# Attention scores of one transformer layer on one core: two score blocks at a time, with the product of high parts done as two half-height matmuls

## The chip, the cores and the metric

The kernel runs on one core of a Trainium2 chip. A core has a matrix engine (PE; its weight loads are listed apart as PEld), a vector engine (DVE), a scalar engine (ACT), a small general engine (POOL), and a sequencer (SP) that does nothing here but issue DMAs. Each works through its own list of instructions in order, and they wait for each other by semaphores. PE reads its operands from the 128 partitions of the on-chip memory and writes its results into banks of 128 partitions by 512 float32.

The metric is the device time of one execution, in microseconds (us). Before the change it is 1014.34 us, the median of three runs (1014.22 to 1014.41).

## The reference

One layer with 1024 tokens and a width of 1024, all in float32, cut to what matters here:

```python
hn = rmsnorm(x, norm_mix)
qa, ka, va, qb, kb, vb = split(hn @ w_in)          # head size 64
# A: 8 query heads in 2 groups, one key head a group; |i - j| <= 128
s = q_i @ k_i.T / 8                                 # a block of 128 queries, up to 384 keys
s = where(valid, s, -1e30); m = max(max(s), sink)
p = exp(s - m); o = (p @ v) / (sum(p) + exp(sink - m))
# B: 8 heads over a 16 x 64 grid of tokens, window 8 x 16, learned bias
p = softmax(q_r @ k_win / 8 + bias); o = p @ v_win
h = x + concat(rmsnorm(o_a), rmsnorm(o_b)) @ w_out
h = h + (silu(conv3(rmsnorm(h) @ w_gate)) * (rmsnorm(h) @ w_up)) @ w_down
out = rmsnorm(h)
```

## The kernel before

**Numbers in two parts.** PE multiplies numbers of a reduced float32 format (`fp32r`). To keep float32's precision, a number is split into a high part, which is the number in that format, and a low part, which is the rest. A product of two matrices of 128 rows is then three matmuls: high by high, low by high, high by low (`block`, lines 190 to 192, on the tiles `xgh`, `xgl`, `whi`, `wlo`). A head is only 64 numbers deep, half of PE's 128 rows. So for the scores one tile holds high and low part of the same 64 rows on top of each other: a query tile `q` has high above low, the key tile `ka` one of the two orders and `kb` the other. Two full-height matmuls of `q` with the two key tiles, added up in one bank, give high by high, low by low, high by low and low by high.

**Stages.** The projections `hn @ w_in` run as 18 jobs (`Project`), and eight jobs (`OutA`) are the first half of the output projection. Beside these jobs runs the attention: first A (16 units: 2 groups by 8 blocks of 128 queries), then B (8 heads, each in 4 units with 8 blocks in all). After it come the rest of the output projection, and the gated MLP with its products in a seven-product scheme, to the end.

**What a score goes through.** `scores` (line 397) takes a bank of tag `s`, of which there are two, and issues the two matmuls of line 404 for one block of 128 queries of one head: 384 key columns, or 256 for the first and the last block. `softmax` (line 423) follows: DVE reads the bank, adds mask or bias, and takes the row's extreme `nm` (line 435, called the eviction below: when it ends, the bank is free); ACT takes the exponential (line 443); DVE the reciprocal of the sum (line 445); POOL scales (line 447). Two blocks share one tile `p` and one reciprocal: in A they are two query heads of one group on the same block, in B two neighbouring blocks of one head. Later, `t_step` transposes `p` on PE (lines 483 and 559), ACT and DVE split it (lines 457 and 458), and `v_step` multiplies by the values (lines 489, 490, 570, 571).

**Order.** PE's order is written out by hand. A loop over the units emits transposes, score steps (`q_step`) and value steps, with scores about two units ahead, and after each of them a number of projection blocks set by the table `RATES`. The other engines' order is made by a scheduler from priorities, so that it moves when the code does.

**Stacks.** In B, `split_qk` (line 307) scales and splits a tile that has 64 rows of queries above 64 rows of keys into `ka` (high) and `kb` (low). DMAs on SP's queue then copy the two query parts into `q` (lines 316 and 317), after which the freed upper halves of `kb` and `ka` are overwritten with the keys' high and low parts (lines 318 and 319). In A, `split_first`, `split_pair`, `split_first_k` and `split_k` do the like; there the two query heads of a pair already have their parts stacked in opposite orders, except in `split_pair`.

Of the kernel before, what the change touches and what calls it, by code (L numbers as in the profile page):

```python
# [58 lines left out]
def hybrid_layer(tc, xT, w_first, w_in, w_out, w_gate, w_up, w_down, small, sink, rpb, consts, rope, out):  # L59
    nc = tc.nc  # L60
    with ExitStack() as ctx:
# [32 lines left out]
        f32 = lambda ap: ap.bitcast(F32)  # L94
# [184 lines left out]
        def split_pair(t):  # L279

            a, b = big("q", "op", F32R), big("q", "op", F32R)
            lo = t[:, :].bitcast(F32R)
            for h in range(2):
                nc.scalar.activation(a[:, tsl(h)], t[:, tsl(h)], AF.Copy, scale=-HD ** -0.5)
                nc.vector.scalar_tensor_tensor(lo[:, tsl(h)], t[:, tsl(h)], -HD ** -0.5, f32(a[:, tsl(h)]), op0=ALU.mult, op1=ALU.subtract)
            nc.sync.dma_start(f32(b[0:64, :]), f32(a[64:128, :]))
            nc.sync.dma_start(f32(b[64:128, :]), t[64:128])
            nc.sync.dma_start(f32(a[64:128, :]), t[0:64])
            return [a, b]

# [17 lines left out]
        def split_qk(t):  # L308

            a, b, q = big("ka", "op", F32R), big("kb", "op", F32R), big("q", "op", F32R)  # L310
            by = cst[:, K_SCALE:K_SCALE + 1]
            for h in range(2):
                nc.scalar.activation(a[:, tsl(h)], t[:, tsl(h)], AF.Copy, scale=by)
                nc.vector.scalar_tensor_tensor(b[:, tsl(h)], t[:, tsl(h)], by, f32(a[:, tsl(h)]), op0=ALU.mult, op1=ALU.subtract)
            with tc.high_priority(offset=500):
                nc.sync.dma_start(f32(q[0:64, :]), f32(a[0:64, :]))
                nc.sync.dma_start(f32(q[64:128, :]), f32(b[0:64, :]))
                mark["stacked"] = nc.sync.dma_start(f32(b[0:64, :]), f32(a[64:128, :]))
                nc.sync.dma_start(f32(a[0:64, :]), f32(b[64:128, :]))
            return q, (a, b)  # L320

        def split_k(t, e):

            a, b = big("ka", "op", F32R), big("kb", "op", F32R)
            o = 64 - e
            nc.scalar.activation(a[e:e + 64], t[e:e + 64], AF.Copy)
            nc.sync.dma_start(f32(b[o:o + 64, :]), f32(a[e:e + 64, :]))
            nc.vector.tensor_tensor(b[e:e + 64], t[e:e + 64], f32(a[e:e + 64, :]), op=ALU.subtract)
            nc.sync.dma_start(f32(a[o:o + 64, :]), f32(b[e:e + 64, :]))
            return a, b  # L330

        later = []

# [61 lines left out]
        def near(b):  # L395
            return [c for c in (b - 1, b, b + 1) if 0 <= c < NB]

        def scores(q, k, b):
            cs = near(b)
            n = 128 * len(cs)  # L400
            ps = bank("s", "s")
            qs = q[:, b * 128:(b + 1) * 128]
            for i in range(2):
                nc.tensor.matmul(ps[:, 0:n], qs, k[i][:, cs[0] * 128:cs[0] * 128 + n].rearrange("p (s w) -> p w s", s=2), start=i == 0, stop=i == 1)  # L404
            return ps, n

        pairs = [0]
        w2 = lambda ap: ap.rearrange("p (s w) -> p s w", s=2)

# [10 lines left out]
                with tc.high_priority(offset=50):  # L420
                    deferred.pop(0)(*order)

        def softmax(st, j, ps, n, bias, nsink=None):

            exponentials()
            w = lambda ap: ap.rearrange("p (s w) -> p s w", s=2)
            p = st["p"]
            with tc.high_priority(offset=50):
                nm = spool.tile([128, 1], F32, name="nm")
                if j == 0:  # L430
                    st["sm"], st["n"] = spool.tile([128, 2], F32, name="sm"), [n, n]
                sm, st["n"][j] = st["sm"], n
                if nsink is not None and j == 0:
                    nc.gpsimd.tensor_copy(p[:, 0:2, n:n + 1], nsink.rearrange("p (j o) -> p j o", o=1))
                nc.vector.tensor_tensor_reduce(  # L435
                    out=w(p[:, j, 0:n]), in0=ps[:, 0:n].rearrange("p (w s) -> p s w", s=2), in1=bias, scale=1.0, scalar=3e38 if nsink is None else nsink[:, j:j + 1],
                    op0=ALU.add, op1=ALU.min, accum_out=nm)
                e = n if nsink is None else n + 1
                widths = list(st["n"])

                def finish(*order):
                    with behind(*order):
                        nc.scalar.activation(p[:, j, 0:e], p[:, j, 0:e], AF.Exp, bias=nm, scale=-1.0, accum_out=sm[:, j:j + 1])  # L443
                    if j == 1:
                        nc.vector.reciprocal(sm, sm)  # L445
                        for i, m in enumerate(widths):
                            mark["scaled"] = nc.gpsimd.tensor_scalar(p[:, i, 0:m], p[:, i, 0:m], sm[:, i:i + 1], 1.0, op0=ALU.mult, op1=ALU.mult)  # L447

                deferred.append(finish)
                if nsink is None:  # L450
                    exponentials()
# [9 lines left out]
        def unit_window(g, b):  # L461

            cs, n = near(b), 128 * len(near(b))
            ps4 = [None] * 4
            mask = w2(cst[:, K_MA + 128 * (cs[0] - b + 1):K_MA + 128 * (cs[-1] - b + 2)])
            st = {}

            def q_step(j):
                def go():
                    if j % 2 == 0:  # L470
                        st["p"] = pair_tile(True)
                    ps, _ = scores(qa[g, j // 2][j % 2], ka[g], b)
                    softmax(st, j % 2, ps, n, mask, nsink[:, 4 * g + j - j % 2:4 * g + j - j % 2 + 2])
                    ps4[j] = st["p"][:, j % 2, :]
                return go

            def t_step(i):
                def go():
                    if i == 0:
                        st["o"] = bank("o", "o")  # L480
                    pt = bank("pt", "pt")
                    for j in range(4):
                        nc.tensor.transpose(pt[:, j * 128:(j + 1) * 128], ps4[j][:, i * 128:(i + 1) * 128], ident)  # L483
                    ph, pl = split_pt(pt, HALF)
                    exponentials("high")

                    def v_step():
                        o, v = st["o"], va[g]
                        nc.tensor.matmul(o, v[:, cs[i], :], mv(ph[:, :]), start=i == 0, stop=False)
                        nc.tensor.matmul(o, v[:, cs[i], :], mv(pl[:, :]), start=False, stop=i == len(cs) - 1)  # L490
                        if i == len(cs) - 1:
                            leave()
                    return v_step
                return go

            def leave():
                ot = apool.tile([128, 2, 128], F32, name="ot", tag="ot", bufs=1, padded_shape=[128, 4, 128])
                o4 = pv(st["o"][:, :])
                halved = lambda ap: ap.rearrange("p (s w) -> p s w", s=2)
                for e in range(2):  # L500
                    me, other = slice(64 * e, 64 * e + 64), slice(64 - 64 * e, 128 - 64 * e)
                    nc.scalar.activation(ot[me].rearrange("p j (s w) -> p j s w", s=2), o4[other, e::2], AF.Copy)
                    for i in range(2):
                        if mix[2 * g + i] is None:
                            mix[2 * g + i] = big("mixa", "mix")
                        nc.vector.tensor_tensor(halved(mix[2 * g + i][me, b * 128:(b + 1) * 128]), o4[me, e + 2 * i], halved(ot[me, i, :]), op=ALU.add)

            return [q_step(j) for j in range(4)], [t_step(i) for i in range(len(cs))]
# [20 lines left out]
        def units_grid(h):  # L529
# [6 lines left out]
            def q_step(b):  # L536
                def go():
                    if b == 0:
                        bias_of[h] = bias_of.pop(h, None) or bias_tiles(h)
                    if b == 4 and h < 7:  # L540
                        bias_of[h + 1] = bias_tiles(h + 1)
                    x = bias_of[h]
                    if b % 2 == 0:
                        st["p"] = pair_tile()
                    sel = slice(2, 5, 2) if b == 0 else slice(0, 3, 2) if b == NB - 1 else slice(1, 4)
                    ps, n = scores(qb[h], kb[h], b)
                    softmax(st, b % 2, ps, n, x[:, sel, :] if n == 256 else w2(x[:, sel, :].rearrange("p c w -> p (c w)")))
                    ps4[b] = st["p"][:, b % 2, :]
                return go
# [1172 lines left out]
```

## Time and profile before

| | before |
|---|---|
| median of three runs | 1014.34 us (1014.22 to 1014.41) |
| span of the profiled execution | 1012.1 us |
| outside the span (difference of these two) | 2.2 us |
| PE busy | 1004.5 us, 99% of the span |
| weight loads, DVE, ACT, POOL busy | 88%, 82%, 55%, 10% |
| granted clock of PE | 0.998 of full |
| score matmuls (line 404) | 256, from 52.1 to 330.4 us |

The profile comes from one execution, of which the span from the first to the last instruction is known; nothing else of that execution's own time is given, so the span stands for it. A timeline row gives start, length, engine, line, operation and tiles. PE's matmuls overlap in their pipeline and the ends given are modelled: a row of 0.38 us is followed by the next one 0.22 us later. So what a matmul costs is read from the distance between two starts, not from the length. A "busy" of 99% says likewise only that PE's list never ran dry.

### The profile page before, as it was taken

Reading aid. Unit: us, or ns where it says so; the run is one execution under the profiler, and the core shown is the slowest. Engines: PE = TensorE matmul, PEld = TensorE weight load, DVE = VectorE, ACT = ScalarE, POOL = GpSimd, SP = SyncE. Lnnn points to the kernel's source line nnn. Section 1 sums busy time; section 2 is a strip of 40 time slices with the busy share of each in tenths; the row PEclk is TensorE's granted clock in tenths of the full one; section 3 lists DMA queues with packets and bytes.
Section 4 is the critical chain, followed back from the end, with each engine's and each line's share of the span. In section 5 each row is a group of like instructions: output and inputs, shape, how many; then the busy total and the mean of one; then the engine's idle time right before and its main releaser. Section 6 shows DMA issues by size and latency. Waiting matters only on the chain.

```text
span 1012.1 us, 14835 instructions
## 1 busy us (share of the span) xinstructions
PE 1004.5 (99%) x5080; PEld 888.4 (88%) x5080; DVE 834.7 (82%) x1570; ACT 561.0 (55%) x1080; POOL 101.6 (10%) x186
## 2 busy tenths in 40 slices
PE   9999999999999999999999999999999999999997
PEld 8899898899899888888888888888888888888887
DVE  7899887768888799999987786786777678996675
ACT  8567776658687554565544443443444645554451
POOL 0233342222322100000000000000000000000001
PEclk9999999999999999999999999999999999999999
DMA  7223022333334366232552333323332799976654
GB/s 296 83 79 90 32 73 63 84 84 83 95 94 136 126 205 220 74 103 64 195 187 90 112 115 115 105 94 115 104 119 90 239 315 329 306 241 231 214 174 177
DMA packets 68524, 145.46 MB, mean 144 GB/s; under 512 B 8280, under 2 KB 18784, under 8 KB 68448
## 3 DMA queue, kind: packets, MB, share of 16 engines
q1 hardware_dynamic: 58360, 119.27, 36.9%
q10 hardware_dynamic: 10088, 25.24, 6.4%
q8 instruction: 40, 0.66, 0.3%
q14 instruction: 36, 0.29, 0.1%
HBM read 104.11 MB, written 28.58 MB: 131 GB/s over the span
## 4 chain that ended last, share of the span: by engine, by line
PE 93%; DVE 3%; ACT 2%; DMA 1%; issue 1%; SPq 0%; DVEq 0%; ACTq 0%
PE x L1059 8%; PE x L1057 8%; PE x L1058 8%; PE pj L190 7%; PE pj L192 7%; PE pj L191 7%; PE dn L1059 7%; PE dn L1058 7%; PE dn L1057 7%; PE y L1059 4%; PE y L1057 4%; PE y L1058 4%; PE s L404 3%; PE pt L483 2%; PE z L1057 2%; PE z L1059 2%
## 5 line engine op out<-in xcount | busy, mean ns | idle before, releaser
L1057 PE MATMUL x<-hg,whi 128*128 128x512 f32 x352 | 133.5, 379 | 0.0
L1058 PE MATMUL x<-hg,whi 128*128 128x512 f32 x352 | 133.4, 379 | 0.0
L1059 PE MATMUL x<-hg,wlo 128*128 128x512 f32 x352 | 133.4, 379 | 0.0
L1057 PE MATMUL dn<-xd,whi 128*128 128x512 f32 (+1 forms) x330 | 120.8, 366 | 0.0
L1058 PE MATMUL dn<-xd,whi 128*128 128x512 f32 (+1 forms) x330 | 120.5, 365 | 0.0
L1059 PE MATMUL dn<-xd,wlo 128*128 128x512 f32 (+1 forms) x330 | 120.5, 365 | 0.0
L1031 ACT ACTIVATE whi<-ws 128x512 fp32r<-128x512 f32 (+1 forms) x100 | 60.9, 623 | 76.0 <-DVE ws L1171 14.5
L443 ACT ACTIVATE p<-p,nm 128x385 f32<-128x385 f32 (+3 forms) x128 | 75.2, 588 | 45.8 <-DVE nm L435 43.1
L190 PE MATMUL pj<-xgh,whi 128*128 128x512 f32 x245 | 99.7, 407 | 0.2 <-DVE v L346 0.2
L447 POOL TENSOR_SCALAR p<-p,sm 128x384 f32<-128x384 f32 (+1 forms) x128 | 76.4, 610 | 195.9 <-DVE sm L445 161.7
L191 PE MATMUL pj<-xgl,whi 128*128 128x512 f32 x245 | 92.9, 379 | 0.0
L192 PE MATMUL pj<-xgh,wlo 128*128 128x512 f32 x245 | 92.9, 379 | 0.0
L1031 ACT ACTIVATE whi<-raw 128x512 fp32r<-128x512 f32 (+1 forms) x102 | 61.2, 612 | 49.9 <-PE x L1058 14.9
L1032 DVE TENSOR_TENSOR wlo<-ws,whi 128x512 fp32r<-128x512 f32 (+1 forms) x100 | 66.8, 683 | 20.0 <-ACT whi L1031 19.6
L458 DVE TENSOR_TENSOR pl<-pt,ph 128x384 fp32r<-128x384 f32 (+2 forms) x108 | 63.4, 587 | 17.5 <-ACT ph L457 16.5
L1057 PEld LDWEIGHTS x<-hg,whi 128*128 128x128 f32 x352 | 66.5, 189 | 9.4
L1058 PEld LDWEIGHTS x<-hg,whi 128*128 128x128 f32 x352 | 66.5, 189 | 9.4
L1059 PEld LDWEIGHTS x<-hg,wlo 128*128 128x128 f32 x352 | 66.5, 189 | 9.4
L1032 DVE TENSOR_TENSOR wlo<-raw,whi 128x512 fp32r<-128x512 f32 (+1 forms) x102 | 66.8, 672 | 6.2 <-ACT whi L1031 6.1
L1532 POOL TENSOR_TENSOR h<-h,wide 128x256 f32<-128x256 f32 x4 | 2.8, 731 | 671.2 <-ACT wide L1528 671.2
L457 ACT ACTIVATE ph<-pt 128x384 fp32r<-128x384 f32 (+2 forms) x108 | 55.4, 513 | 26.3 <-PE pt L483 14.2
L1057 PEld LDWEIGHTS dn<-xd,whi 128*128 128x128 f32 x330 | 62.5, 189 | 7.8
(276 smaller groups left out, 2504.2 us busy)
## 6 DMA issues: line engine op xcount, KB each, us to landing
xd<-x SPq DMA_DIRECT2D x77, 256.0 KB, 4.9
raw<-in_w_down_dram SPq DMA_DIRECT2D x72, 256.0 KB, 4.6
raw<-in_w_gate_dram SPq DMA_DIRECT2D x22, 512.0 KB, 3.5
raw<-in_w_up_dram SPq DMA_DIRECT2D x22, 512.0 KB, 3.8
x<-c ACTq DMA_DIRECT2D x22, 512.0 KB, 2.8
raw<-in_w_in_dram SPq DMA_DIRECT2D x30, 256.0 KB, 2.8
raw<-in_w_down_dram SPq DMA_DIRECT2D x36, 192.0 KB, 4.2
x<-t ACTq DMA_DIRECT2D x11, 512.0 KB, 2.6
```

What stands on the lines that cost most here:

```text
L190: nc.tensor.matmul(ps, w[0], mv(x[0][:, tsl(h)]), start=first, stop=False)
L191: nc.tensor.matmul(ps, w[0], mv(x[1][:, tsl(h)]), start=False, stop=False)
L192: nc.tensor.matmul(ps, w[1], mv(x[0][:, tsl(h)]), start=False, stop=last)
L443: nc.scalar.activation(p[:, j, 0:e], p[:, j, 0:e], AF.Exp, bias=nm, scale=-1.0, accum_out=sm[:, j:j + 1])
L447: mark["scaled"] = nc.gpsimd.tensor_scalar(p[:, i, 0:m], p[:, i, 0:m], sm[:, i:i + 1], 1.0, op0=ALU.mult, op1=ALU.mult)
L457: mark["high"] = nc.scalar.activation(ph[:, 0:n], ps[:, 0:n], AF.Copy)
L458: mark["rest"] = nc.vector.tensor_tensor(pl[:, 0:n], ps[:, 0:n], f32(ph[:, 0:n]), op=ALU.subtract)
L1031: nc.scalar.activation(hi, src, AF.Copy)
L1032: nc.vector.tensor_tensor(lo, src, f32(hi[:, :, :]), op=ALU.subtract)
L1057: nc.tensor.matmul(ps, w[0], x[0], start=first and i == 0, stop=False, skip_group_check=True)
L1058: nc.tensor.matmul(ps, w[0], x[1], start=False, stop=False, skip_group_check=True)
L1059: nc.tensor.matmul(ps, w[1], x[0], start=False, stop=last and i == len(ws) - 1, skip_group_check=True)
```

## The change

The changed kernel makes the scores of two blocks together. For the two, high by high is done with two matmuls that use only 64 of the 128 rows: the first block's with partitions 0 to 63, the second's with partitions 64 to 127, each into its own bank. Then each block gets one full-height matmul that adds high by low and low by high. So two blocks take two half-height and two full-height matmuls where they took four full-height ones. The product of the low parts, which is far below the others, is left out.

For this the second block's queries must be stacked the other way (low above high). In A `split_pair` now does so, and `split_k` returns its tiles in the other order. In B both blocks belong to one head, so `q` is filled block by block: even blocks high above low, odd blocks low above high. That takes four DMAs for a head where there were two, each of half the bytes, in pieces of 128 columns. Odd score steps in A do nothing now; in B they do only the softmax of a score made one step earlier. In A the second softmax of two no longer flushes the waiting exponentials first (`flush`).

```diff
@@ split_pair @@
-            nc.sync.dma_start(f32(b[0:64, :]), f32(a[64:128, :]))
-            nc.sync.dma_start(f32(b[64:128, :]), t[64:128])
+            nc.sync.dma_start(f32(b[64:128, :]), f32(a[64:128, :]))
+            nc.sync.dma_start(f32(b[0:64, :]), t[64:128])
@@ split_qk @@
-                nc.sync.dma_start(f32(q[0:64, :]), f32(a[0:64, :]))
-                nc.sync.dma_start(f32(q[64:128, :]), f32(b[0:64, :]))
+                by_block = lambda x: f32(x).rearrange("p (b w) -> p b w", w=128)
+                for r, high, low in ((slice(0, 64), 0, 1), (slice(64, 128), 1, 0)):
+                    for x, first in ((a, high), (b, low)):
+                        nc.sync.dma_start(by_block(q[r, :])[:, first::2], by_block(x[0:64, :])[:, first::2])
@@ split_k @@
-            return a, b
+            return b, a
@@ instead of scores @@
-        def scores(q, k, b):
-            cs = near(b)
-            n = 128 * len(cs)
-            ps = bank("s", "s")
-            qs = q[:, b * 128:(b + 1) * 128]
-            for i in range(2):
-                nc.tensor.matmul(ps[:, 0:n], qs, k[i][:, cs[0] * 128:cs[0] * 128 + n].rearrange("p (s w) -> p w s", s=2), start=i == 0, stop=i == 1)
-            return ps, n
+        def scores_of_two(q, k, blocks):
+            out = []
+            for e, b in enumerate(blocks):
+                cs = near(b)
+                at, n = cs[0] * 128, 128 * len(cs)
+                out.append((bank("s", "s"), q[e][:, b * 128:(b + 1) * 128],
+                            [t[:, at:at + n].rearrange("p (s w) -> p w s", s=2) for t in k], n))
+            for e, r in enumerate((slice(0, 64), slice(64, 128))):
+                ps, qs, ks, n = out[e]
+                nc.tensor.matmul(ps[:, 0:n], qs[r], ks[e][r], start=True, stop=False)
+            for e in range(2):
+                ps, qs, ks, n = out[e]
+                nc.tensor.matmul(ps[:, 0:n], qs, ks[1 - e], start=False, stop=True)
+            return [(ps, n) for ps, _, _, n in out]
@@ softmax @@
-        def softmax(st, j, ps, n, bias, nsink=None):
-            exponentials()
+        def softmax(st, j, ps, n, bias, nsink=None, flush=True):
+            if flush:
+                exponentials()
@@ unit_window, q_step @@
-                    if j % 2 == 0:
-                        st["p"] = pair_tile(True)
-                    ps, _ = scores(qa[g, j // 2][j % 2], ka[g], b)
-                    softmax(st, j % 2, ps, n, mask, nsink[:, 4 * g + j - j % 2:4 * g + j - j % 2 + 2])
-                    ps4[j] = st["p"][:, j % 2, :]
+                    if j % 2:
+                        return
+                    st["p"] = pair_tile(True)
+                    both = scores_of_two(qa[g, j // 2], ka[g], (b, b))
+                    for e in range(2):
+                        softmax(st, e, both[e][0], n, mask, nsink[:, 4 * g + j:4 * g + j + 2], e == 0)
+                        ps4[j + e] = st["p"][:, e, :]
@@ units_grid, q_step @@
                     if b % 2 == 0:
                         st["p"] = pair_tile()
+                        st["both"] = scores_of_two((qb[h], qb[h]), (kb[h][1], kb[h][0]), (b, b + 1))
-                    ps, n = scores(qb[h], kb[h], b)
+                    ps, n = st["both"][b % 2]
```

In the changed file the half-height matmuls are on line 426, the full-height ones on line 429; the eviction is on line 445, the reciprocal on 455, the transposes of A on 495, the value matmuls of A on 501 and 502, the split of `pt` on 468.

**PE's list, in A.** The place is group 0, block 6, its first two heads. A row is line, operation, tiles (out<-in) and shape. Before, the two heads' scores stand apart:

```order
L192 MATMUL pj<-xgh,wlo 128x512
L404 MATMUL s<-ka,q 128x384
L404 MATMUL s<-kb,q 128x384
L489 MATMUL o<-ph,v 128x512
L490 MATMUL o<-pl,v 128x512
L190 MATMUL pj<-xgh,whi 128x512
L191 MATMUL pj<-xgl,whi 128x512
L192 MATMUL pj<-xgh,wlo 128x512
L404 MATMUL s<-ka,q 128x384
L404 MATMUL s<-kb,q 128x384
L483 MATMUL pt<-cst,p 128x128 x4
```

With the change, in the same place:

```order
L192 MATMUL pj<-xgh,wlo 128x512
L426 MATMUL s<-ka,q 128x384
L426 MATMUL s<-kb,q 128x384
L429 MATMUL s<-kb,q 128x384
L429 MATMUL s<-ka,q 128x384
L501 MATMUL o<-ph,v 128x512
L502 MATMUL o<-pl,v 128x512
L190 MATMUL pj<-xgh,whi 128x512
L191 MATMUL pj<-xgl,whi 128x512
L192 MATMUL pj<-xgh,wlo 128x512
L495 MATMUL pt<-cst,p 128x128 x4
```

The second head's scores moved ahead, past two value matmuls and three of a projection; all else keeps its order and its number.

**DVE's list, in A.** The place is group 0, block 7, where scores have 256 columns; an `ISA` row that writes `p,nm` is an eviction, the one behind it reads out its row extreme. Before:

```order
L458 TENSOR_TENSOR pl<-pt,ph 128x512
L445 RECIPROCAL sm<-sm 128x2
L435 ISA p,nm<-s,cst,nsink 128x256
L435 ISA nm 128x1
L506 TENSOR_TENSOR mixa<-o,ot 64x128 x2
L435 ISA p,nm<-s,cst,nsink 128x256
L435 ISA nm 128x1
L506 TENSOR_TENSOR mixa<-o,ot 64x128 x2
L258 TENSOR_TENSOR t<-pj,rstd_336 128x8x8x8
L458 TENSOR_TENSOR pl<-pt,ph 128x512
L445 RECIPROCAL sm<-sm 128x2
L435 ISA p,nm<-s,cst,nsink 128x256
```

With the change:

```order
L468 TENSOR_TENSOR pl<-pt,ph 128x512
L445 ISA p,nm<-s,cst,nsink 128x256
L445 ISA nm 128x1
L445 ISA p,nm<-s,cst,nsink 128x256
L445 ISA nm 128x1
L183 TENSOR_TENSOR wlo<-raw,whi 128x512
L518 TENSOR_TENSOR mixa<-o,ot 64x128 x2
L468 TENSOR_TENSOR pl<-pt,ph 128x512
L258 TENSOR_TENSOR t<-pj,rstd_336 128x8x8x8
L455 RECIPROCAL sm<-sm 128x2
L445 ISA p,nm<-s,cst,nsink 128x256
L445 ISA nm 128x1
```

The two evictions of a pair now follow each other, and the work that stood between them comes behind both.

**SP's list, at the seventh head of B.** Before:

```order
L316 DMA q<-ka 64x1024
L317 DMA q<-kb 64x1024
L319 DMA ka<-kb 64x1024
L318 DMA kb<-ka 64x1024
L175 DMA raw<-in_w_out_dram 128x512
```

With the change:

```order
L319 DMA q<-ka 64x4x128 x2
L319 DMA q<-kb 64x4x128 x2
L321 DMA ka<-kb 64x1024
L320 DMA kb<-ka 64x1024
L175 DMA raw<-in_w_out_dram 128x512
```

Four copies into `q` now stand ahead of the two that overwrite the tiles they read.

## The prediction

> **What bounds the kernel now.** I read the page's totals and its chain first, then the stages.
>
> ```profile
> span 1012.1 us, 14835 instructions
> PE 1004.5 (99%) x5080; PEld 888.4 (88%) x5080; DVE 834.7 (82%) x1570; ACT 561.0 (55%) x1080; POOL 101.6 (10%) x186
> PE 93%; DVE 3%; ACT 2%; DMA 1%; issue 1%; SPq 0%; DVEq 0%; ACTq 0%
> ```
>
> PE is busy for 99% of the span and carries 93% of the chain that ended last. So time taken out of PE's list moves the end, as long as nobody else becomes late. Whether someone would is read by stage. The windows are attention A, attention B, and the rest; the columns are PE, PEld, DVE, ACT, POOL, granted clock, DMA.
>
> ```profile
> 52.00:180.00 128.00, 128.00 (x729) 114.83 (x728) 111.64 (x327) 94.00 (x240) 43.98 (x92) 1.00 0.25 67
> 180.00:331.00 151.00, 150.76 (x886) 136.57 (x885) 125.10 (x314) 106.61 (x259) 45.06 (x72) 1.00 0.37 97
> 331.00:1012.00 681.00, 675.08 (x3230) 592.49 (x3228) 555.47 (x872) 325.47 (x538) 4.58 (x7) 1.00 0.48 165
> ```
>
> In both attention stages PE never runs dry and has its full clock; DVE is next, at 111.64 / 128 = 87% and 125.10 / 151 = 83%. So the change works on the bound. The score matmuls by shape, with the MLP's 512-column matmul for comparison:
>
> ```profile
> L1057 PE MATMUL x<-hg,whi 128*128 128x512 f32 x352 | 133.5, 379 | 0.0
> L404 PE MATMUL s<-ka,q 128*128 128x384 f32 x96 | 32.7, 340 | 0.0
> L404 PE MATMUL s<-kb,q 128*128 128x384 f32 x96 | 31.3, 326 | 0.0
> L404 PE MATMUL s<-ka,q 128*128 128x256 f32 x32 | 9.3, 291 | 0.0
> L404 PE MATMUL s<-kb,q 128*128 128x256 f32 x32 | 8.8, 275 | 0.0
> ```
>
> These are 82 us by the lengths, but lengths overlap. The price is the distance between starts, here at a score of each width:
>
> ```profile
> 144.05 0.38 PE L192 MATMUL pj<-xgh,wlo 128*128 128x512 f32 x1
> 144.26 0.33 PE L404 MATMUL s<-ka,q 128*128 128x384 f32 x1
> 144.43 0.33 PE L404 MATMUL s<-kb,q 128*128 128x384 f32 x1
> 144.59 0.38 PE L489 MATMUL o<-ph,v 128*128 128x512 f32 x1
> ...
> 163.12 0.27 PE L404 MATMUL s<-ka,q 128*128 128x256 f32 x1
> 163.23 0.28 PE L404 MATMUL s<-kb,q 128*128 128x256 f32 x1
> 163.34 0.38 PE L489 MATMUL o<-ph,v 128*128 128x512 f32 x1
> ```
>
> A 512-column matmul costs 0.21 to 0.22 us, a 384-column one 0.33 / 2 = 0.163, a 256-column one 0.11. All scores together cost 192 x 0.163 + 64 x 0.11 = 38 us, not 82.
>
> **What the change removes.** For two blocks, four slots of PE become three if the two half-height matmuls run at the same time, since the pair then lasts as long as its longer half. The slot saved is the shorter half's. There are 128 blocks, so 64 pairs. In A both halves have one width: 6 inner blocks x 4 pairs = 24 of 384, and 2 outer blocks x 4 = 8 of 256. In B the first and the last pair of each head mix 256 and 384: 16 pairs with a shorter half of 256, and 16 of 384. That is 40 x 0.163 + 24 x 0.11 = 6.5 + 2.6 = **9.1 us**. The bound from the other side is no overlap at all: the same four slots, 0 us. I take the full overlap; why, stands with the rivals.
>
> **What it adds: weight loads.** Every matmul has its own load; four for a pair stay four, now in three slots. The loads of the first score above, and a score behind transposes:
>
> ```profile
> 144.05 0.19 PEld L404 LDWEIGHTS s<-ka,q 128*128 128x128 f32 x1
> 144.27 0.19 PEld L404 LDWEIGHTS s<-kb,q 128*128 128x128 f32 x1
> ...
> 77.47 0.60 PE L483 MATMUL pt<-cst,p 128*128 128x128 f32 x4
> 77.80 0.19 PEld L404 LDWEIGHTS s<-ka,q 128*128 128x128 f32 x1
> 77.83 0.41 PE L404 MATMUL s<-ka,q 128*128 128x384 f32 x1
> 77.91 0.19 PEld L404 LDWEIGHTS s<-kb,q 128*128 128x128 f32 x1
> 78.08 0.33 PE L404 MATMUL s<-kb,q 128*128 128x384 f32 x1
> ```
>
> A load starts with the matmul before its own (144.05, 144.27), and the next can start 0.11 us later (77.80, 77.91). Behind a 512-column matmul there are 0.216 us, room for both half loads at 2 x 0.11, so those cost nothing; by the changed order 51 pairs stand there. The other 13 stand behind transposes, which have distances of (0.60 - 0.27) / 3 = 0.11 us, room for one load. There the second half starts up to 0.11 us late: 13 x 0.11 = **1.4 us**, at the least 0 if both halves load at once. The two full-height loads hide under the 0.163 or 0.11 us of the matmul before them, as today.
>
> **What it moves: the two banks.** A pair needs both `s` banks free, so it waits for the later of two evictions where a score waited for the one two steps back. Behind it on PE wait projections and value matmuls. The tightest place before, at the block where DVE's list is shown above:
>
> ```profile
> 100.01 0.27 PE L404 MATMUL s<-ka,q 128*128 128x256 f32 x1
> ...
> 102.27 0.47 DVE L435 CUSTOM_DVE_ANT_0 p<-s,cst,nsink 128x256 f32<-128x256 f32 x1
> ...
> 102.80 0.19 PEld L404 LDWEIGHTS s<-ka,q 128*128 128x128 f32 x1 [0.40 <-DVE nm L435]
> ...
> 103.06 0.47 DVE L435 CUSTOM_DVE_ANT_0 p<-s,cst,nsink 128x256 f32<-128x256 f32 x1
> ```
>
> The eviction came 2.26 us after its score, and the score at 102.80 had already waited for it. As a pair it needs the second eviction too, which now follows directly: 102.27 + 2 x 0.47 = 103.2, some 0.5 us late. I carried this out for all pairs: end of the first eviction, plus the second's length, against the next pair's start less the 0.15 us that the pair before saves. Five places come out late, by 1.9 us in all, the largest here and at 182.3; the second of these is at B's start; after it pairs in B lie about 5 us apart and nothing waits. Since A's evictions move ahead of other DVE work, I take **1.5 us**; the bounds are 0 and, with DVE at 111.64 / (128 - 5) = 91% in A and every place slightly worse, 4.
>
> **What it moves: the stacks in B.** Each head has four copies where there were two, ahead of the two that put the keys in place. Least room has the seventh head, whose first score starts at 294.85:
>
> ```profile
> 286.12 0.47 SPq L316 DMA_DIRECT2D q<-ka  x1
> 286.96 0.47 SPq L317 DMA_DIRECT2D q<-kb  x1
> 289.13 0.46 SPq L319 DMA_DIRECT2D ka<-kb  x1
> 290.32 0.46 SPq L318 DMA_DIRECT2D kb<-ka  x1
> ...
> 294.85 0.27 PE L404 MATMUL s<-ka,q 128*128 128x256 f32 x1
> ```
>
> The key copies wait for the query copies that read the same tile to land (about 3 us, 286.12 to 289.13). Two more issues of 0.47 us put the last query copy of each tile 0.5 to 0.9 us later, so the last key copy issues near 291 and lands near 294, just before the score. Cost 0; without that cover up to 1 us, at this head alone. ACT, DVE and POOL do the same operations as before.
>
> **Sum.** 9.1 - 1.4 - 1.5 = 6.2 us off a span of 1012.1. The span lies 2.2 us under the runs' median, and I take that part as unchanged: 1014.3 - 6.2 = **1008.1 us**. After 331 us nothing changes but the start; there DVE is at 555.47 / 681 = 82%, and the stage is taken to shift as a whole.
>
> **Rivals.**
>
> *The second half's load comes late.* If a load may start only when the matmul just ahead of it in the list starts, as every load quoted does, the second half starts 0.11 us behind the first. Then 384-column pairs save 0.163 - 0.11 = 0.05 us and the others nothing: 40 x 0.05 = 2, less 1.5 for the banks: 1013.8. For it speaks the lockstep of 144.05 and 144.27. Against it: the lockstep is just as well explained by one spare set of weights for all 128 rows, which is taken over at that moment; a half-height load needs only its half of that set, and the other half's is free. The trace can't decide; the second reading gives a reason for the moment seen, so I hold it for likelier. The Trainium skill ("TensorE: Matmul & The Clock Gate", Part 3) states that loads for other row groups are pulled ahead and that matmuls on different rows start about 4 ns apart; no run here shows it yet, and by it the sum would be the forecast.
>
> *No overlap.* The halves run one after the other, or only the weights do less: 0 saved, 1.5 for the banks, 1015.8. No row speaks for it, none against.
>
> *Slower: the array must run empty whenever a matmul with another number of rows follows.* Each pair changes to half height and back, 128 changes in all. A matmul's row is 379 ns long and the next starts after 216, so what is left in the pipe is 0.163 us; emptying it 128 times costs 20.9 us, and the time is 1008.1 + 20.9 = 1029. Slower than before from 6.2 / 128 = 0.05 us a change. The nearest rows are the one kind of matmul that isn't 128 by 128:
>
> ```profile
> 986.87 0.38 PE L1059 MATMUL dn<-xd,wlo 128*128 128x512 f32 x1
> 987.09 0.27 PE L1513 MATMUL row<-cst,v 128*4 128x128 f32 x1
> 987.12 0.46 PE L1057 MATMUL dn<-xd,whi 128*128 128x512 f32 x1
> 987.42 0.38 PE L1058 MATMUL dn<-xd,whi 128*128 128x512 f32 x1
> ```
>
> It starts 0.22 us after its forerunner, on time, and the second one after it 0.33 later, which is one load (0.11) and one matmul (0.22). So going to 4 columns and back cost no emptying; but that is columns, not rows. The Trainium skill ("TensorEngine Tiling (Array Packing)", Key Properties) states that changing the tiling mode drains the engine. These rows do not show it, and they alone would not settle it for rows.
>
> **How the numbers follow.** Chances: forecast 0.57, late load 0.15, no overlap 0.10, emptying or another slowing 0.18. A measurement of this kernel can tell about 0.2%, 2.0 us, from no change. The forecast's own range is 1005.2 (9.1 saved, nothing lost) to 1010.6 (bank waits at 4); all of it is faster. Late load and no overlap are within 0.2%, but for late loads without bank waits (1012.3), at the edge. Faster is 0.57 + 0.04 = 0.61; the same 0.21; slower 0.18. The range goes from 1005 up to 1016, past no overlap, and leaves out the emptying.
>
> **What would show it.** Right: the two rows of a half-height pair start within 0.02 us of each other, the first full-height one 0.16 (or 0.11) later; starts from the first half to the matmul behind the pair are 0.49 us apart at 384 columns, not 0.65. Late load: the halves start 0.11 apart and their loads stand in lockstep with the matmuls. No overlap: 0.16 apart. Emptying: the first half starts clearly more than 0.22 behind its 512-column forerunner, or the first full one late. Bank waits: idle time before line 426 released by the eviction's `nm`, 1 to 2 us, nearly all in A. Stacks: PE waits for a DMA at the seventh head. The forecast is wrong if DVE in A turns out the bound, with PE waiting for evictions pair after pair, or if the stage after 331 us keeps its old end.

## The result, and the profile after

The changed kernel takes 1030.07 us (median of four runs, 1030.03 to 1030.93) against 1014.28 us before: a ratio of 1.0161, 95% interval 1.0147 to 1.0176. It is 15.8 us slower, where 6.2 us less was forecast. The page's totals and chain after, to be laid beside those of before:

```profile
span 1028.2 us, 14867 instructions
PE 1020.3 (99%) x5080; PEld 877.6 (85%) x5080; DVE 836.2 (81%) x1570; ACT 556.1 (54%) x1080; POOL 104.0 (10%) x186
PE 94%; DVE 2%; ACT 2%; issue 1%; DMA 1%; SPq 0%; DVEq 0%; ACTq 0%
```

The span grew by 16.1 us and PE's busy time by 15.8, with the same 5080 matmuls. So the time is on PE itself, and no other engine became the bound. The stages, cut where B's first transposes and the last scores stand now (columns as in the prediction: PE, PEld, DVE, ACT, POOL, clock, DMA):

```profile
52.00:187.00 135.00, 135.00 (x724) 108.51 (x723) 112.20 (x324) 90.06 (x237) 43.45 (x92) 1.00 0.24 63
187.00:347.00 160.00, 159.50 (x890) 132.11 (x889) 126.71 (x320) 105.66 (x261) 49.05 (x72) 1.00 0.33 93
347.00:1028.00 681.00, 675.20 (x3233) 593.09 (x3231) 555.18 (x870) 325.55 (x538) 3.88 (x6) 1.00 0.48 165
```

A takes 135 us instead of 128, B 160 instead of 151, the rest 681 as before. PE is listed as busy through both attention stages, yet the weight loads fill less of them: in A 108.51 us of 135 where it was 114.83 of 128. That is the first hint: loads stand still while PE counts as busy.

One pair shows the rest. PE's matmuls and its weight loads (PEld), from the timeline, at a pair of 384 columns:

```profile
99.20 0.38 PE L192 MATMUL pj<-xgh,wlo 128*128 128x512 f32 x1
99.51 0.43 PE L426 MATMUL s<-ka,q 64*128 64x384 f32 x1
99.51 0.43 PE L426 MATMUL s<-kb,q 64*128 64x384 f32 x1
99.87 0.43 PE L429 MATMUL s<-kb,q 128*128 128x384 f32 x1
100.14 0.33 PE L429 MATMUL s<-ka,q 128*128 128x384 f32 x1
100.30 0.38 PE L501 MATMUL o<-ph,v 128*128 128x512 f32 x1
```

```profile
98.99 0.19 PEld L192 LDWEIGHTS pj<-xgh,wlo 128*128 128x128 f32 x1
99.51 0.18 PEld L426 LDWEIGHTS s<-ka,q 64*128 64x128 f32 x1 [0.33 <-issue]
99.51 0.18 PEld L426 LDWEIGHTS s<-kb,q 64*128 64x128 f32 x1
99.87 0.19 PEld L429 LDWEIGHTS s<-kb,q 128*128 128x128 f32 x1 [0.17 <-issue]
99.98 0.19 PEld L429 LDWEIGHTS s<-ka,q 128*128 128x128 f32 x1
```

Both halves start at 99.51, and their records are 3 to 4 ns apart, here and in 61 of the 64 pairs: they do run side by side. But the first starts 0.31 us behind the 512-column matmul of 99.20, which needs 0.216. The 0.09 us between I read as an array that runs empty; the rows show the pause, not what happens inside the array. And the first half's load, which should have begun at 99.20, begins only at 99.51 too, so that its 0.11 us stand bare, with no matmul to cover them. The same happens on the way back: 99.51 + 0.11 (load) + 0.163 (384 columns) = 99.78, and the full-height load starts at 99.87, 0.09 us later, again with nothing to cover it. From 99.20 to 100.30 it is 1.10 us; before, a 512-column matmul and four scores took 0.216 + 4 x 0.163 = 0.87. A pair costs 0.23 us more, not 0.16 less.

So a **change of height** costs 0.09 + 0.11 = 0.20 us. 128 of them are 25.6 us, the overlap gives back 9.1: 16.5 us by this count, 15.8 measured. The waits of three pairs, shown further down, would add 1.4 us, so the count is good to some 2 us and no better.

### The profile page after: what moved, and what is told of

It reads as the page before. It is cut to its first block, busy times and chain, and to the rows that moved or that the text cites. A ratio compares the mean times of both kernels' runs of the same rounds, so it can differ in the third digit from the quotient of the medians.

```text
span 1028.2 us, 14867 instructions
## 1 busy us (share of the span) xinstructions
PE 1020.3 (99%) x5080; PEld 877.6 (85%) x5080; DVE 836.2 (81%) x1570; ACT 556.1 (54%) x1080; POOL 104.0 (10%) x186
## 4 chain that ended last, share of the span: by engine, by line
PE 94%; DVE 2%; ACT 2%; issue 1%; DMA 1%; SPq 0%; DVEq 0%; ACTq 0%
PE x L1072 7%; PE x L1071 7%; PE x L1070 7%; PE pj L190 7%; PE pj L192 7%; PE pj L191 7%; PE dn L1070 6%; PE dn L1071 6%; PE dn L1072 6%; PE y L1072 4%; PE y L1071 4%; PE y L1070 4%; PE s L429 3%; PE s L426 2%; PE pt L495 2%; PE z L1072 2%
## 5 line engine op out<-in xcount | busy, mean ns | idle before, releaser
L1401 ACT ACTIVATE xd<-xd 128x512 fp32r<-128x512 f32 x77 | 47.3, 625 | 40.5 <-DMA xd<-x 40.3
```

## The experiments

**The theory**: the number of rows decides; each change of it makes PE pause (the array runs empty) and holds back the next load. **The rivals**: waits for the two banks and for B's stacks, which moved too; or a cost that sticks to every half-height matmul, whatever stands beside it.

### Full height again, everything else as changed

```diff
-            for e, r in enumerate((slice(0, 64), slice(64, 128))):
-                ps, qs, ks, n = out[e]
-                nc.tensor.matmul(ps[:, 0:n], qs[r], ks[e][r], start=True, stop=False)
-            for e in range(2):
-                ps, qs, ks, n = out[e]
-                nc.tensor.matmul(ps[:, 0:n], qs, ks[1 - e], start=False, stop=True)
+            for i in range(2):
+                for e in range(2):
+                    ps, qs, ks, n = out[e]
+                    nc.tensor.matmul(ps[:, 0:n], qs, ks[e if i == 0 else 1 - e], start=i == 0, stop=i == 1)
```

> The changed kernel's order, stacks and pairs, but high by high again as full-height matmuls (with the product of low parts): four full-height matmuls for a pair. Theory (each change of height on PE empties the array, 0.09 us, and leaves the next weight load uncovered, 0.11 us; 128 changes cost 25.6 us, the side-by-side halves give back 9.1): no change of height is left, so 1014.3 plus at most 2 for the banks that a pair waits for. Rival (the loss comes from the moved order: waits for the two banks, late stacks): it stays, and the fourth slot comes back on top, 1030.1 + 9.1 = 1039.

Measured: 1017.56 us, 1.0032 times before (1.0020 to 1.0043). The order and the stacks are not the main cause: with them and without changes of height most of the loss is gone, although a slot came back. What is left, 3.3 us, is more than the 2 allowed. The waits of PE and of its loads in this run, as sum, count and longest:

```profile
PE s L427 <- DMA kb<-ka: 1.3, 2, 0.7
PE o L582 <- DVE pl L466: 0.6, 1, 0.6
...
PEld s L427 <- DVE nm L443: 1.5, 5, 0.4
```

```profile
297.17 0.35 PE L427 MATMUL s<-kb,q 128*128 128x256 f32 x1 [0.71 <-DMA kb<-ka]
...
317.23 0.35 PE L427 MATMUL s<-kb,q 128*128 128x256 f32 x1 [0.62 <-DMA kb<-ka]
```

1.5 us is the wait for banks, over five places, as the loads have it; 1.3 us is the wait for the keys of B's seventh and eighth heads.

### Half, full, half, full

```diff
             for e, r in enumerate((slice(0, 64), slice(64, 128))):
                 ps, qs, ks, n = out[e]
                 nc.tensor.matmul(ps[:, 0:n], qs[r], ks[e][r], start=True, stop=False)
-            for e in range(2):
-                ps, qs, ks, n = out[e]
                 nc.tensor.matmul(ps[:, 0:n], qs, ks[1 - e], start=False, stop=True)
```

> The changed kernel with a pair's four matmuls in the order half, full, half, full: four changes of height in a pair where there were two, and no halves side by side. Theory (0.20 us a change): 128 more changes cost 25.6 us and the lost overlap 9.1: 1030.1 + 34.7 = 1065. Rival (a fixed cost for each pair or for each half-height matmul, whatever stands beside it): only the lost overlap, 1039.

Measured: 1062.73 us, 1.0481 times before (1.0466 to 1.0495). Twice the changes and no overlap: 32.7 us above the changed kernel, where 34.7 was reckoned for the changes and the lost overlap together, and 9 for the rival. The cost follows the number of changes.

```profile
102.16 0.38 PE L192 MATMUL pj<-xgh,wlo 128*128 128x512 f32 x1
102.47 0.43 PE L426 MATMUL s<-ka,q 64*128 64x384 f32 x1
102.83 0.43 PE L427 MATMUL s<-kb,q 128*128 128x384 f32 x1
103.19 0.43 PE L426 MATMUL s<-kb,q 64*128 64x384 f32 x1
103.55 0.43 PE L427 MATMUL s<-ka,q 128*128 128x384 f32 x1
103.81 0.38 PE L499 MATMUL o<-ph,v 128*128 128x512 f32 x1
```

Inside the pair every start is 0.36 us behind the one before: 0.163 for the columns, 0.20 for the change.

### All of a pair at half height

```diff
-            for e, r in enumerate((slice(0, 64), slice(64, 128))):
-                ps, qs, ks, n = out[e]
-                nc.tensor.matmul(ps[:, 0:n], qs[r], ks[e][r], start=True, stop=False)
-            for e in range(2):
-                ps, qs, ks, n = out[e]
-                nc.tensor.matmul(ps[:, 0:n], qs, ks[1 - e], start=False, stop=True)
+            for i in range(3):
+                for e, r in enumerate((slice(0, 64), slice(64, 128))):
+                    ps, qs, ks, n = out[e]
+                    nc.tensor.matmul(ps[:, 0:n], qs[r], ks[1 - e if i == 1 else e][r], start=i == 0, stop=i == 2)
```

> The changed kernel with all matmuls of a pair at half height: three times two side by side, the first block always on partitions 0 to 63, the second on 64 to 127. In place of low by high it computes high by high once more, so the scores are not the reference's; the work on PE is that of a full set. Three slots and two changes of height for a pair, as in the changed kernel. Theory (the cost belongs to the change): 1030, and inside the pair the second and third two start 0.16 us after those before them, with their loads covered. Rival (a half-height load is never covered and a half-height matmul always starts from an empty array): two more such steps of 0.20 us in each of 64 pairs, 1030 + 25.6 = 1056.

Measured: 1032.12 us, 1.0173 times before (1.0159 to 1.0187). Six half-height matmuls with two changes cost 2.1 us more than two of them with two changes, not 26; the rival's 1056 is out. Rows that print as one (x2) hide the single starts, so the loads show it:

```profile
98.06 0.18 PEld L427 LDWEIGHTS s<-ka,q 64*128 64x128 f32 x1 [0.33 <-DVE t L258]
98.07 0.29 PEld L427 LDWEIGHTS s<-kb,q 64*128 64x128 f32 x2
98.17 0.34 PEld L427 LDWEIGHTS s<-ka,q 64*128 64x128 f32 x2
98.34 0.19 PEld L427 LDWEIGHTS s<-kb,q 64*128 64x128 f32 x1
98.75 0.19 PEld L499 LDWEIGHTS o<-ph,v 128*128 128x128 f32 x1 [0.22 <-ACT ph L465]
```

Six loads run between 98.06 and 98.53 with no gap inside: at one height the next loads are covered. Only the first and the return (98.75) stand bare. The releasers named there (`t`, `ph`) change from pair to pair; for most the list names none (`issue`), and the pause is there at every pair.

### Both halves on the same rows

```diff
-            for e, r in enumerate((slice(0, 64), slice(64, 128))):
+            for e in range(2):
+                r = slice(0, 64)
                 ps, qs, ks, n = out[e]
```

> The changed kernel with both half-height matmuls of a pair on partitions 0 to 63, so that they can't run side by side; two changes of height for a pair as in the changed kernel. The second block's rows there are the low part of its queries, so its scores are not the reference's; the work on PE is the same. Theory (the halves truly overlap in the changed kernel, and that gives back 9.1 us): 1030.1 + 9.1 = 1039, with the two starts 0.16 us apart, or 0.11. Rival (starts 4 ns apart are only how the record is made, and the halves run one after the other there too): 1030.

Measured: 1038.00 us, 1.0234 times before (1.0220 to 1.0248), 7.9 us above the changed kernel. The overlap is real; by this measure it is worth some 8 us, where 9.1 was reckoned.

```profile
97.89 0.38 PE L192 MATMUL pj<-xgh,wlo 128*128 128x512 f32 x1
98.20 0.43 PE L427 MATMUL s<-ka,q 64*128 64x384 f32 x1
98.46 0.32 PE L427 MATMUL s<-kb,q 64*128 64x384 f32 x1
98.72 0.43 PE L430 MATMUL s<-kb,q 128*128 128x384 f32 x1
```

On the same rows the second half starts 0.26 us later: the first one's bare load (0.11) and its columns.

### Columns against rows

The prediction held emptying for unlikely because a matmul of 4 columns (line 1513) had come and gone without it. Two runs repeat that shape 128 times in the kernel before, once on 128 rows, once on 64:

```diff
+            nc.tensor.transpose(ps[0:4, 0:128], ones[:, 0:4], ident)
             for i in range(2):
```

> The kernel before with one extra transpose of four columns (128 rows, 4 columns, the shape of line 1513) ahead of every score, into the bank that the score then overwrites: 128 of them. If a change in columns costs nothing, as the one in line 1513 seemed to: 0.11 us each (one more load in the row), 1014.3 + 14 = 1028, and each starts 0.22 us behind a 512-column forerunner. If a change in columns empties the array as a change in rows does: two changes of 0.20 us and the matmul itself, 0.05, for each: 128 x 0.45 = 58, 1072.

Measured: 1028.39 us, 1.0138 times before (1.0123 to 1.0154): 0.11 us for each, one load.

```diff
+            nc.tensor.transpose(ps[0:4, 0:64], ones[0:64, 0:4], ident[0:64, 0:64])
             for i in range(2):
```

> The run with the extra four-column transposes once more, but each of them on 64 rows instead of 128 (64 rows, 4 columns, 64 numbers streamed): the same count, the same places, no score changed. Theory (a change in the number of rows empties the array and uncovers the next load, a change in columns does not): each costs 2 x 0.09 for emptying, some 0.05 for itself and its own load, and 0.11 for the uncovered load behind it, 0.33 us: 1014.2 + 128 x 0.33 = 1056, and it starts 0.31 us behind a 512-column forerunner, not 0.22. Rival (what costs is the kind of work, the reduced float format at half height or the two row groups at once, and not the number of rows as such): 1028, as with 128 rows.

Measured: 1056.79 us, 1.0424 times before (1.0406 to 1.0441): 0.33 us for each. Half the rows, three times the price. First the run with 128 rows, then the one with 64:

```profile
144.56 0.38 PE L192 MATMUL pj<-xgh,wlo 128*128 128x512 f32 x1
144.77 0.27 PE L403 MATMUL s<-cst,ones 128*4 128x128 f32 x1
144.80 0.41 PE L405 MATMUL s<-ka,q 128*128 128x384 f32 x1
145.05 0.33 PE L405 MATMUL s<-kb,q 128*128 128x384 f32 x1
```

```profile
146.78 0.38 PE L192 MATMUL pj<-xgh,wlo 128*128 128x512 f32 x1
147.09 0.21 PE L403 MATMUL s<-cst,ones 64*4 64x64 f32 x1
147.23 0.43 PE L405 MATMUL s<-ka,q 128*128 128x384 f32 x1
147.50 0.33 PE L405 MATMUL s<-kb,q 128*128 128x384 f32 x1
```

0.21 us behind the forerunner with 128 rows, 0.31 with 64. The stream is plain float32 here, one transpose at a time, no two halves, and the place, the count and the bank are the same in both runs. Only the number of rows differs and, with it, the numbers streamed (64 instead of 128), which make the matmul shorter and not dearer. So the rows do it.

### A alone, with half height

The kernel before, with the diff's edits of A (`scores_of_two`, `split_pair`, `split_k`, `q_step` of `unit_window`, `flush`) and none of B's:

```diff
+                    both = scores_of_two(qa[g, j // 2], ka[g], (b, b))
...
                     ps, n = scores(qb[h], kb[h], b)
```

> The kernel before with attention A alone changed, half-height matmuls and all; B as before. Theory (0.20 us a change, additive): 64 changes cost 12.8, the 24 pairs of 384 and 8 of 256 columns give back 24 x 0.163 + 8 x 0.11 = 4.8, so 1014.1 + 8.0 = 1022, and little for banks, since PE is later. Rival (a cost that belongs to B, with its mixed widths and new stacks): 1014 to 1016.

Measured: 1021.81 us, 1.0075 times before (1.0061 to 1.0089). 7.6 us for half of the pairs: the cost adds up, and A's part answers to its 7 us in the windows.

### The two moved things apart

A by twos at full height, B as before (`scores_of_two` of the first experiment, in A only):

> The kernel before with attention A alone scored by twos, with full-height matmuls (and the product of low parts); B and its stacks as before. Theory (what is left when the changes of height are gone, 3.3 us, is about 2 us of waits for the two banks in A and 1.3 us for B's keys): 1014.1 + 2 = 1016. Rival (it comes from B alone, from the stacks): 1014.

Measured: 1014.84 us, 1.0004 times before (0.9996 to 1.0013), which is not told from no change. And the four stacking copies alone, in the kernel before:

```diff
-                nc.sync.dma_start(f32(q[0:64, :]), f32(a[0:64, :]))
-                nc.sync.dma_start(f32(q[64:128, :]), f32(b[0:64, :]))
+                by_block = lambda x: f32(x).rearrange("p (b w) -> p b w", w=128)
+                for r, high, low in ((slice(0, 64), 0, 1), (slice(64, 128), 1, 0)):
+                    for x, first in ((a, high), (b, low)):
+                        nc.sync.dma_start(by_block(q[r, :])[:, first::2], by_block(x[0:64, :])[:, first::2])
```

> The kernel before with B's queries stacked block by block by four DMAs for a head, and nothing else; the full-height matmuls give the same scores from either order. Prediction's term: hidden, 1014.1, at most 1 more at the seventh head. Rival (from the wait for the keys' copies seen with the fourth slot back): PE waits for them at one or two heads, 1.3 us, 1015.4.

Measured: 1014.10 us, 1.0001 times before (0.9992 to 1.0010). A by twos was expected at 1016, the stacks at 1014.1 or, by the rival, at 1015.4: alone, neither costs anything that can be told from noise. So the 3.3 us of the first experiment come only with B's pairs, which were not run without the new stacks; whether it takes both is not shown. The lists above put 1.3 of them on the keys of two heads and 1.5 on banks. Why the keys come late stays open.

## Why the prediction was wrong

The bound was read rightly: PE's list sets the end, the stages before and after attention only shift, and every experiment moved the span by what it moved in PE's busy time, within 1.3 us.

**The step that failed** is the price of a change of height, which stands in the sum at nothing; the runs give it 0.20 us, 128 times, 25.6 us. That is a choice among the rivals: "The array must run empty whenever a matmul with another number of rows follows" was written down as the slower side, with a chance of 0.18, and a stop at every such change is what happens. It was held down by one row, the four-column matmul at 987.09, with the caveat that "that is columns, not rows"; the runs show that the caveat was the whole matter, 0.11 us against 0.33 for the same matmul. The Trainium skill ("TensorEngine Tiling (Array Packing)", Key Properties) says that a change of tiling mode drains the engine. For rows the traces agree, with 0.09 us a change. The matmul of four columns shows no drain; whether four columns count as another mode no run here shows.

**Its price** was near the result by two errors that cancel. Emptying was put at 0.163 us, from a matmul's modelled length less its distance to the next; it is 0.09, 12 us in all and not 20.9. But the load held back with it was not seen: 0.11 us on each of 128 changes, 14 us. "The two full-height loads hide under the 0.163 or 0.11 us of the matmul before them, as today" is wrong for the first of the two, and the half loads behind a 512-column matmul, put at nothing, stand bare as well. That the rival's 1029 lies so near the measured 1030.07 is luck. The prediction's lead, "a load starts with the matmul before its own", holds only while the height stays the same.

**The terms of the sum.** The overlap, put at 9.1 us, held: 3 to 4 ns between the halves, as the forecast and the Trainium skill ("TensorE: Matmul & The Clock Gate", Part 3) had it, and about 8 us by the run on the same rows. The 1.4 us for a second half load behind transposes is 0: there too the two halves start together, as behind the transposes of 129.03, so the rival of the late load falls.

```profile
129.56 0.43 PE L426 MATMUL s<-kb,q 64*128 64x384 f32 x1
129.56 0.43 PE L426 MATMUL s<-ka,q 64*128 64x384 f32 x1
```

The banks were put at 1.5 us and the stacks at 0, at most 1. In the changed kernel the second half starts clearly behind the first in three pairs, at 91.25, 191.64 and 329.63. The rows of the last two, PE's but for the load of 191.64:

```profile
191.16 0.43 PE L426 MATMUL s<-kb,q 64*128 64x384 f32 x1
191.64 0.18 PEld L426 LDWEIGHTS s<-ka,q 64*128 64x128 f32 x1 [0.29 <-DVE nm L445]
329.41 0.35 PE L426 MATMUL s<-kb,q 64*128 64x256 f32 x1 [0.45 <-DVE mixb L600]
```

At 191.64 and at 91.25 the second half waits for the second bank: the eviction before it ends at 191.58 and at 91.18, 0.06 and 0.07 us earlier. By the distances to the matmul behind the pair these two cost 0.45 and 0.20 us, so the banks took 0.65 us. One of the two is the place at B's start that the prediction named; the other it named, the tightest before, no longer waits. At 329.41, the first pair of B's eighth head, the list names a vector operation that the score does not read. The last copy of that head's keys was issued at 323.57 and took 5.8 us to land, until 329.37, against 3.2 us for the seventh head's: the pair waits for its keys, by this reading, and is 0.71 us late. So the stacks' term held in size, with the seventh head's place taken by the eighth. With full-height pairs it was 1.3, and alone it could not be told from nothing.

## What to carry to other kernels

Matmuls of half the rows run side by side, but entering and leaving half height cost 0.40 us together here, because PE pauses and the next weights are not loaded ahead. One saved slot of 384 columns is 0.163 us, so a visit would have to hold 0.40 / 0.163 = 2.5 such pairs, that is three, to pay (an estimate from these rows; with two score banks there is room for one). Before trusting a row that seems to show a switch to be free, repeat that very switch in a run of its own: the number of rows and the number of columns behave differently.

## What was not expected of the hardware

Changing the columns of the stationary operand (128 to 4 and back) costs nothing beyond its load, 128 times over, while changing its rows (128 to 64) costs a pause of 0.09 us and an uncovered load each way. Two loads on different halves of the rows start within 0.01 us of each other; on the same rows the second follows 0.11 us later:

```profile
98.19 0.18 PEld L427 LDWEIGHTS s<-ka,q 64*128 64x128 f32 x1 [0.33 <-issue]
98.30 0.19 PEld L427 LDWEIGHTS s<-kb,q 64*128 64x128 f32 x1
```

These are the loads of the run with both halves on the same rows.
